# The mixer's input projection as 28 Strassen pairs in a stage of its own, with the delta rule beside the keys, the key fold and half the output projection

## The chip, the cores and the metric

The kernel runs on one NeuronCore of one Trainium2 chip. The metric is the time of one execution in microseconds (us). Time before: a median of 2743.02 us over three runs (2742.67 to 2745.15). TensorE (PE) multiplies matrices into PSUM, VectorE (DVE) and ScalarE (ACT) work on elements, GpSimd (POOL) does some element work and issues DMAs from software, SyncE (SP) issues DMAs. Each engine works through its own instructions in order and waits for the others by semaphores.

## What is computed

One layer of a streaming encoder on 512 tokens of width 2048, in float32: a token mixer, cross-attention to 256 memory tokens, and a feed-forward block with a short convolution. Cut to what matters here:

```python
h = rmsnorm(x, mix_norm)
proj = h @ w_mix_in                   # q, k, v, z (1024 each), 16 gate columns, 3 x 1024 of the short convolution
qkv = silu(causal_dwconv(proj[..., :3 * W], conv_w))
o = gated_delta_rule(l2norm(q), l2norm(k), v, g, beta)          # 8 heads x 128
y_gdn = rmsnorm(o, out_gain) * silu(z)
y_sc = b_gate * causal_dwconv(c_gate * h2, sc_conv)             # 1024 channels
x = x + concatenate([y_gdn, y_sc]) @ w_mix_out
x = x + memory_xattn(rmsnorm(x), rmsnorm(mem), w_q, w_k, w_v, w_o)
x = x + conv_ffn(rmsnorm(x), w_up, ffn_conv, w_down)
return rmsnorm(x, final_norm)
```

The delta rule carries a state of 128 x 128 for each head over the tokens. It is computed in chunks, with a unit lower triangular system to be solved in each. The kernel takes chunks of 128 tokens, four for each head.

## The kernel before

**Precision.** A float32 operand is split into a rounded part hi (type fp32r) and a rest lo. `wpiece` loads a piece of weights of 128x1024 (512 KB) on SP's queue, casts it on ScalarE (L143) and subtracts on VectorE (L144). `mm3` multiplies with three matmuls (hi hi, hi lo, lo hi; L154 to L156). Where the moving operand has only 256 columns, its hi and lo stand side by side in 512: one matmul over 512 columns and one over 256 then do the same (`mm2s`, L169 and L172).

**Stages**, in the order in which TensorE meets them:

1. `mem_proj(w_xk)`: keys of the memory tokens. The first pieces are loaded in parts by a hand-written order.
2. The key fold: `w_xq` times the keys, so that scores later need one product. The result goes to `wk_d`. The loads of x (POOL's queue) and its sums of squares stand beside it.
3. `mem_proj(w_xv)`: values, with the norm of x beside it.
4. The output fold: values times `w_xo`, to `mo_d`. Beside it the normed x is split into `hs`, and `gate_rows` computes the gate columns.
5. The mixer's input projection: 56 tiles of 128 columns. `wproj` gives each 16 x 3 matmuls over 512 columns. Four tiles for each head (`qkvz`), then 24 tiles for the short convolution.
6. The mixer's output projection, 16 tiles with K = 2048 (`proj`).
7. Scores and softmax; the attention's output (`out_proj`), with `up_prepare` beside it, which makes the seven operands of stage 8.
8. The up-projection in 44 Strassen pairs: two tiles of weights times both halves of the tokens, K in two halves. Seven products of 8 x (512 + 256) columns stand for eight of 8 x 3 x 256. The sums of weights are made in part by accumulating DMAs on POOL's queue (`pair_loads`), in part on VectorE.
9. The down-projection, also in Strassen form, and the final norm.

**The delta rule** of a head is a generator, `delta(h, ...)`. `weave` puts it on a list, and `tick` runs after every three matmuls of `wproj`: it adds 0.65 us to a written clock and takes the next step of each chain whose delay has passed. A step yields its own cost on TensorE and the delay until the next. So the order of the delta's matmuls among the products is fixed when the program is written, by these estimates. A head treats its four chunks at once in one tile of 128x512; a chunk's diagonal blocks of 32x32 are inverted by 31 steps of substitution on VectorE (L612, L613), over 128 partitions and 4 columns each (`G = 8` groups), with a round trip through memory before (`nd_d`) and after (`xd_d`), both on SP's queue. The recurrence then goes through the four chunks with tiles of 128x128. Outside of regions marked `manual_schedule`, a list scheduler orders the instructions of each engine by their place in the program and by their operands' readiness.

**Buffers.** 64 tiles of 128x512 (`tp`), five raw pieces of weights (`WST`), three of each split part, eight PSUM banks (3 `PM`, 5 `PG`).

## Time and profile before

| what | us |
|---|---|
| median of three runs | 2743.02 |
| the profiled execution | 2746.9 |
| its span, first to last instruction | 2745.1 |
| granted TensorE clock, mean | 0.998 |
| TensorE busy | 2719.1 |
| VectorE busy | 2101.1 |
| ScalarE busy | 1422.3 |
| the mixer's input projection (372 to 1078 us of the span) | 706.0 |
| the up-projection (1441 to 2308 us) | 867.0 |

Busy times are those of the trace; a matmul's mean duration (0.39 us for 512 columns) overlaps with the next one's, so that spacings are read from start to start.

### The profile page before, as it was taken

The page shows a single profiled execution, that of the slowest core. Times are in us where ns is not written, and L with a number is a line of the kernel's source. Part 1 is how long each engine was busy: PE and PEld are TensorE (multiplying, and loading weights), DVE is VectorE, ACT ScalarE, POOL GpSimd, SP SyncE. Part 2 cuts the span into 40 slices and gives each one's busy share as a digit, 9 for nine tenths or more (in the row PEclk, how much of TensorE's full clock was granted, in tenths as well). Part 3 has the DMA queues.
Part 4 walks back from the last instruction along what each step waited for, and adds up shares of the span by engine and source line. Part 5 has one row for each costly group of instructions (what it writes and reads, how often), then busy time and mean ns, then how long its engine had stood idle before and what let it go on. Part 6 is the DMA issues. An engine that isn't in the chain of part 4 may idle for free.

```text
span 2745.1 us, 38051 instructions
## 1 busy us (share of the span) xinstructions
PE 2719.1 (99%) x14045; PEld 2298.6 (84%) x14045; DVE 2101.1 (77%) x3342; ACT 1422.3 (52%) x2086; POOL 267.4 (10%) x258
## 2 busy tenths in 40 slices
PE   9999999999999999999999999999999999999998
PEld 8888788888788888888788888888888888888786
DVE  7777547878775324445679999999999999878878
ACT  6674644345443323224566656565656555554445
POOL 2120001012110000110020000000000000000201
PEclk9999999999999999999999999999999999999999
DMA  7786863333322234445566676767676776864976
GB/s 266 235 292 198 253 197 100 111 96 93 108 92 91 90 102 138 146 150 169 169 177 170 175 198 177 197 170 195 181 193 175 190 186 203 257 190 148 273 252 180
DMA packets 215851, 479.35 MB, mean 175 GB/s; under 512 B 28768, under 2 KB 96112, under 8 KB 215664
## 3 DMA queue, kind: packets, MB, share of 16 engines
q1 hardware_dynamic: 156320, 372.28, 41.9%
q0 software_dynamic: 20272, 62.94, 13.1%
q10 hardware_dynamic: 39072, 41.69, 4.3%
q8 instruction: 110, 1.80, 0.3%
q14 instruction: 77, 0.63, 0.1%
HBM read 424.13 MB, written 52.71 MB: 174 GB/s over the span
## 4 chain that ended last, share of the span: by engine, by line
PE 66%; DVE 2%; DMA 1%; issue 1%; ACT 1%; ACTq 0%; SPq 0%; DVEq 0%
PE px L169 12%; PE px L172 6%; PE pz L169 6%; PE psd L1232 4%; PE psd L1231 4%; PE psd L1230 4%; PE pssc L154 3%; PE psx L155 3%; PE psx L154 3%; PE psx L156 3%; PE pssc L156 3%; PE pssc L155 3%; PE pz L172 3%; PE py L169 3%; PE py L172 1%; PE pss L782 1%
## 5 line engine op out<-in xcount | busy, mean ns | idle before, releaser
L144 DVE TENSOR_TENSOR wlo<-wst,whi 128x1024 fp32r<-128x1024 f32 x316 | 393.0, 1245 | 283.5 <-ACT whi L143 280.4
L143 ACT CAST whi<-wst 128x1024 fp32r<-128x1024 f32 x316 | 331.5, 1049 | 516.0 <-PE pssc L155 143.9
L169 PE MATMUL px<-xo,whi 128*128 128x512 f32 x1400 | 352.7, 394 | 2.9 <-DVE ub L1149 2.9
L169 PEld LDWEIGHTS px<-xo,whi 128*128 128x128 f32 x1400 | 252.8, 190 | 48.9 <-DVE ub L1149 3.1
L863 ACT CAST whi<-wst 128x1024 fp32r<-128x1024 f32 x177 | 185.7, 1051 | 206.7 <-PE pz L169 119.8
L1232 PE MATMUL psd<-wlo,hdh 128*128 128x512 f32 x616 | 241.7, 392 | 3.4 <-DVE wlo L990 3.2
L1230 PE MATMUL psd<-whi,hdh 128*128 128x512 f32 x616 | 240.7, 391 | 0.1
L1231 PE MATMUL psd<-whi,hdl 128*128 128x512 f32 x616 | 240.6, 391 | 0.0
L864 DVE TENSOR_TENSOR wlo<-wst,whi 128x1024 fp32r<-128x1024 f32 x177 | 215.9, 1220 | 1.7 <-ACT whi L863 1.7
L172 PEld LDWEIGHTS px<-xo,wlo 128*128 128x128 f32 x1400 | 191.3, 191 | 13.8
L172 PE MATMUL px<-xo,wlo 128*128 128x256 f32 x1400 | 195.5, 283 | 0.0
L169 PE MATMUL pz<-xo,whi 128*128 128x512 f32 x704 | 176.6, 393 | 0.5 <-ACT whi L863 0.5
L863 ACT CAST whi<-s 128x1024 fp32r<-128x1024 f32 x131 | 136.3, 1040 | 78.3 <-PE px L169 42.6
L987 ACT CAST whi<-wst 128x1024 fp32r<-128x1024 f32 x99 | 104.3, 1053 | 122.8 <-issue 55.2
L864 DVE TENSOR_TENSOR wlo<-s,whi 128x1024 fp32r<-128x1024 f32 x131 | 159.9, 1221 | 0.4 <-ACT whi L863 0.4
L154 PE MATMUL psq<-hh,whi 128*128 128x512 f32 x384 | 155.7, 406 | 0.0
L154 PE MATMUL pssc<-hh,whi 128*128 128x512 f32 x384 | 153.3, 399 | 0.0
L156 PE MATMUL psq<-hh,wlo 128*128 128x512 f32 x384 | 150.3, 391 | 0.0
L156 PE MATMUL pssc<-hh,wlo 128*128 128x512 f32 x384 | 150.0, 391 | 0.0
L155 PE MATMUL psq<-hl,whi 128*128 128x512 f32 x384 | 149.9, 390 | 0.0
L155 PE MATMUL pssc<-hl,whi 128*128 128x512 f32 x384 | 149.8, 390 | 0.0
L169 PEld LDWEIGHTS pz<-xo,whi 128*128 128x128 f32 x704 | 126.6, 189 | 23.2 <-ACT whi L863 0.7
(369 smaller groups left out, 5924.1 us busy)
## 6 DMA issues: line engine op xcount, KB each, us to landing
wst<-in_w_up SPq DMA_DIRECT2D x132, 512.0 KB, 4.1
wst<-in_w_dn SPq DMA_DIRECT2D x121, 512.0 KB, 4.5
wst<-in_w_mix SPq DMA_DIRECT2D x112, 512.0 KB, 3.5
s<-in_w_up POOLq DMA_DIRECT2D x87, 512.0 KB, 6.0
s<-in_w_up SPq DMA_DIRECT2D x43, 512.0 KB, 4.5
hid<-hf_d SPq DMA_DIRECT2D x77, 256.0 KB, 5.2
wst<-in_w_xq SPq DMA_DIRECT2D x32, 512.0 KB, 5.0
wst<-in_w_xv SPq DMA_DIRECT2D x32, 512.0 KB, 3.8
```

The costliest lines, as they stand in the source:

```text
L143: nc.scalar.copy(hi, st)
L144: nc.vector.tensor_tensor(lo, st, f(hi), op=ALU.subtract)
L154: nc.tensor.matmul(ps, wh, xh, start=first, stop=False)
L155: nc.tensor.matmul(ps, wh, xl, start=False, stop=False)
L156: nc.tensor.matmul(ps, wl, xh, start=False, stop=last)
L169: nc.tensor.matmul(ps, hi[:, k * P : (k + 1) * P], x, start=first and k == 0, stop=False, skip_group_check=True)
L172: nc.tensor.matmul(ps[:, n:], lo[:, k * P : (k + 1) * P], x[:, :n], start=False, stop=end, skip_group_check=True)
L863: nc.scalar.copy(hi, t)
L864: nc.vector.tensor_tensor(lo, t, f(hi), op=ALU.subtract)
L1230: nc.tensor.matmul(ps, xh, wh, start=first, stop=False)
L1231: nc.tensor.matmul(ps, xl, wh, start=False, stop=False)
L1232: nc.tensor.matmul(ps, xh, wl, start=False, stop=last)
```

## The change

1. **Order of the stages.** Values first (with the loads and the norm of x beside them), then the output fold, the input projection, and only then keys and key fold, with the delta rule beside these.
2. **The input projection as 28 pairs.** The functions of the up-projection (`up_prepare`, `pair_loads`, the first pair's `begin_parts` and `begin_products`, `quad_left`, `quad_right`) are taken out of stage 8 and used by both. `up_prepare` for the mixer stands beside the output fold. Twelve pairs are those of the short convolution, sixteen those of q, k and v, z of the eight heads. Their results go to memory (`qkvz_d`, `ysc_d`), on ScalarE's queue. No step of the delta rule is woven in here, except for the gates.
3. **The delta rule by chunks of four heads.** A tile holds one chunk of four heads; `prepare_chunk` and `solve` are chains of their own for each of 2 x 4 (half of the heads, chunk), `invert` does the substitution for all 16 blocks of a half at once (`G = 2`, 16 columns on a partition), `recur` the recurrence with tiles of 128x512, `scaled` the norm and the gate. q, k, v, z and the decay are read back from memory on POOL's queue, pieces of 512 bytes, q and k twice.
4. **What it stands beside.** Keys (as before, 16 tiles), the key fold with three matmuls over 256 columns in place of one over 512 and one over 256, and the half of the output projection that needs only the short convolution; its sum with x goes to `xp_d`. The other half comes after the chains.

```diff
-G = 8
+G = 2
...
-    order = [(t, i) for t in tiles for i in range(2)]
...
+    def place(cost):
+        owed[0] += cost
+        if owed[0] > 0.6:
+            due, owed[0] = owed[0], 0.0
+            tick(due)
...
-        kts = mem_proj(g["w_xk"], True)
+        vts = values(g["w_xv"], beside_values)
...
+    def quad_left(pos, blocks, first, *between):
+        if pos:
+            a11, a12, a22, s1, s3 = pair_loads(blocks, pos)
+            w1 = wsplit(a11)
+            px = PG("px")
+            product(px, w1, 1, True)
...
+        product(px, wsplit(s2), 6, False)
...
+        product(pz, wsplit(s1), 5, True)
...
+    def quad_right(pos, left, whole):
+        a12, a22, s2, s3, px, pz, ga, gb, ub = left
+        product(px, wsplit(s3), 7, False)
+        tt(ub, px, ub, op=ALU.add)
...
+        product(pz, wsplit(a12), 3, False)
+        tt(gb, pz, gb, op=ALU.add)
+        if whole:
+            tt(ga[:, HI], gb[:, LO], gb[:, HI], op=ALU.add)
...
+        product(px, wsplit(a22), 4, False)
...
+    for i in range(0, 8, 2):
+        quads += [(40 + i, 48 + i, "ch", i), (41 + i, 49 + i, "ch", i + 1), (32 + i, 33 + i, "b", i)]
+    for h in range(H):
+        quads += [(4 * h, 4 * h + 1, "qk", h), (4 * h + 2, 4 * h + 3, "vz", h)]
...
+    ready_at = (0, 1, 3, 5, 7, 8, 10, 12)
...
+            if step in ready_at:
+                k = ready_at.index(step)
+                if k % 2:
+                    gate_rows(k // 2)
+                up_prepare(xts[k], xts[k + HK])
...
+    for pos, (_, _, kind, i) in enumerate(quads):
...
+        left = quad_left(pos, mix_blocks(pos) if pos else None, first, nothing, run_tails, nothing, nothing)
+        ga, _, ua, _ = quad_right(pos, left, True)
+        left_tail(kind, i, ga, ua)
+        tails.append((kind, i, ga, ua))
+        if pos > 1:
+            next(gate_steps, None)
+    run_tails()
...
+    def prepare_chunk(hb, j):
...
+        gb, k, q = load_decay(hb, j), load4("k", 1, hb, j), load4("q", 0, hb, j)
+        yield 0, 6.0
...
+    def invert(hb):
+        while prepared[hb] < 4:
+            yield 0, 1.0, 0
...
+        for m in range(B - 1):
+            r, n = B - 1 - m, min(m + 1, CB)
...
+            nc.vector.tensor_tensor(t, am, x[:, :n, m : m + 1].broadcast_to([P, n, r]), op=ALU.mult)
+            nc.vector.tensor_tensor(x[:, :n, m + 1 :], x[:, :n, m + 1 :], t, op=ALU.subtract)
+            if m % 4 == 3:
+                yield 0, 5.5, 0
+        nc.sync.dma_start(xd_d[hb].rearrange("j n b (g c) r -> (j n b g) c r", g=G), x)
+        for j in range(4):
+            weave(solve(hb, j), 4.0 + 8.0 * j)
+        weave(recur(hb), 30.0)
...
+            if j:
+                pr = PG("pr")
+                four(pr, ke[i], st)
+                nc.vector.tensor_tensor(r, r, pr, op=ALU.subtract)
+                yield 0.9, 2.5
...
+    order += [g["w_xk"][n, i] for n in range(KT) for i in range(2)]
+    order += [g["w_xq"][i, q] for i in range(KT) for q in range(2)]
+    order += [g["w_mo"][n, 1] for n in range(KT)]
+    for hb in range(2):
+        for j in range(4):
+            weave(prepare_chunk(hb, j), 4.0 + 10.0 * j + hb * 80.0)
+        weave(invert(hb), 20.0 + hb * 85.0)
...
+            for hh in range(2):
+                dst = ps[:, hh * NMEM : (hh + 1) * NMEM]
+                for k in range(4):
...
+                    nc.tensor.matmul(dst, hi[:, c], kt[:, :NMEM], start=k == 0, stop=False, skip_group_check=True)
+                    place(0.12)
+                    nc.tensor.matmul(dst, hi[:, c], kt[:, NMEM:], start=False, stop=False, skip_group_check=True)
+                    place(0.12)
+                    nc.tensor.matmul(dst, lo[:, c], kt[:, :NMEM], start=False, stop=k == 3, skip_group_check=True)
+                    place(0.12)
...
+    yp = [split(loaded(ysc_d[i]), "yp") for i in range(8)]
+    for n in range(KT):
+        ps = out_row(n, yp)
...
+        nc.sync.dma_start(xp_d[n], x0)
     while chains:
         tick(1.0)
...
+    order += [g["w_mo"][n, 0] for n in range(KT)]
+    yp = [split(loaded(y_d[h]), "yp") for h in range(H)]
```

More of the change, by code (lines that the diff above doesn't have):

```diff
@@ L367, in mem_proj, with load_x @@
             held = []
-            if beside:
-                beside(n2)
-        return out
+            beside(n2)
+        return out
+    xacc = cpool.tile([P, S], F32, tag="xacc", name="xacc")
+    xts, r0 = [], []
+    def load_x(n):
+        for _ in range(n):
+            i = len(xts)
+            xts.append(T("x0"))
+            nc.gpsimd.dma_start(xts[i], g["x"][i])
+            add_squares(xacc, xts[i], i == 0)
+    HK = KT // 2
+    S2 = S // 2
+    LO, HI = slice(0, S2), slice(S2, S)
@@ new lines, in gate_rows, with open_pool, TB @@
+    def gate_rows(m):
+        for n, k in enumerate((2 * m, 2 * m + HK, 2 * m + 1, 2 * m + 1 + HK)):
+            nc.tensor.matmul(psba[n * B : (n + 1) * B], wba[:, k], xts[k], start=m == 0, stop=m == 3, skip_group_check=True)
+    tt = nc.vector.tensor_tensor
+    tbs, uss = [], []
+    def open_pool(kept, name, bufs, **more):
+        stack = ctx.enter_context(ExitStack())
+        kept[:] = [stack, stack.enter_context(tc.tile_pool(name=nm(name), bufs=bufs, **more))]
+    def TB(s, dt=F32):
+        return tbs[1].tile([P, S], dt, tag="tb", name=nm(s))
@@ new lines, in begin_parts, with begin_products, some @@
+    def begin_parts(first):
+        a11, a12, a22, s1, s3 = first
+        first += [wsplit(a11), wsplit(a12)]
+        tt(a11, s1, a11, op=ALU.subtract)
+        tt(a12, a12, a11, op=ALU.subtract)
+    def begin_products(first):
+        px, py = PG("px"), PM("py")
+        def some(ps, w, r, low, k0, k1):
+            dst, src = (ps[:, HI], LO) if low else (ps, slice(0, S))
+            for k in range(k0, k1):
+                nc.tensor.matmul(dst, w[low][:, k * P : (k + 1) * P], xop[r][k][:, src], start=low == 0 and k == 0, stop=low == 1 and k == HK - 1, skip_group_check=True)
+        bx, by = (px, first[5], 1), (py, first[6], 2)
+        for args, low, k0 in ((bx, 0, 0), (bx, 1, 0), (by, 0, 0), (bx, 0, HK - 1), (bx, 1, HK - 1), (by, 1, 0), (by, 0, HK - 1), (by, 1, HK - 1)):
+            some(*args, low, k0, HK if k0 else HK - 1)
+        first += [px, py]
@@ new lines, in recur @@
+            vn = T("vn")
+            nc.vector.tensor_tensor(v4(vn), v4(pv), bc(bk[i], P), op=ALU.mult)
+            if 0 < j < 3:
+                sn = T("st")
+                nc.vector.tensor_tensor(v4(sn), v4(st), bc(egl[:, j, H4], P), op=ALU.mult)
+            yield 0.9, 2.5
+            pso = PG("pso")
+            for n in range(4):
+                if j:
+                    nc.tensor.matmul(v4(pso)[:, n], v4(st)[:, n], v4(qd[i])[:, n], start=True, stop=False)
+                nc.tensor.matmul(v4(pso)[:, n], v4(vn)[:, n], v4(at[i])[:, n], start=j == 0, stop=True)
@@ new lines, in trunk @@
+    mws.clear()
+    m2s.clear()
+    for i in range(KT // 2):
+        m2s.append(T("mem"))
+        nc.gpsimd.dma_start(m2s[i].rearrange("p (k m) -> p k m", k=2), g["mem"][2 * i : 2 * i + 2].rearrange("k p m -> p k m"))
+        mem_parts(i)
+    kts = []
+    for n in range(KT):
+        ps = PM("psk")
+        for i in range(2):
+            hi, lo = piece()
+            for k in range(8):
+                nc.tensor.matmul(ps, hi[:, k * P : (k + 1) * P], mws[8 * i + k], start=i == 0 and k == 0, stop=False, skip_group_check=True)
+                place(0.23)
+            for k in range(8):
+                nc.tensor.matmul(ps[:, NMEM:], lo[:, k * P : (k + 1) * P], mws[8 * i + k][:, :NMEM], start=False, stop=i == 1 and k == 7, skip_group_check=True)
+                place(0.12)
+        kts.append(mem_out(ps, 0))
```

736 lines of the change are left out of this document (370 added, 366 removed).

## The prediction

> **What bounds the kernel now.** I read the page's first part, then the busy time by stretch, then what TensorE waited for.
>
> ```profile
> span 2745.1 us, 38051 instructions
> PE 2719.1 (99%) x14045; PEld 2298.6 (84%) x14045; DVE 2101.1 (77%) x3342; ACT 1422.3 (52%) x2086; POOL 267.4 (10%) x258
> ```
>
> TensorE (PE) is busy 99% of the span. Matmuls are pipelined here, so that alone says little; the list of waits says more (engine, line, whom it waited for: total us, times, longest).
>
> ```profile
> PE psd L1232 <- DVE wlo L990: 3.2, 5, 1.6
> PE px L169 <- DVE ub L1149: 2.9, 1, 2.9
> PE pso L670 <- ACT vn L666: 2.7, 1, 2.7
> ...
> PE pv L664 <- DVE cv L661: 1.1, 2, 0.9
> ```
>
> The longest total is 3.2 us in 2745. PE is the bound in every stage, and its time is the number of its instructions times their spacing. The spacing is read from starts, not from mean durations. Here are the stretches (start:end, length, then busy us and count of PE, PEld, DVE, ACT, POOL; granted clock, DMA share, GB/s):
>
> ```profile
> 99.70:190.20 90.50, 90.50 (x515) 78.31 (x515) 68.36 (x98) 67.25 (x113) 25.25 (x26) 1.00 0.91 300
> 190.20:280.00 89.80, 89.80 (x512) 78.64 (x512) 68.27 (x100) 47.18 (x68) 0.00 (x0) 1.00 0.62 199
> 280.00:372.00 92.00, 92.00 (x420) 72.53 (x420) 51.42 (x52) 59.25 (x81) 0.00 (x0) 1.00 0.88 265
> 372.00:794.00 422.00, 418.32 (x2276) 346.45 (x2275) 326.49 (x798) 185.35 (x316) 56.84 (x49) 1.00 0.36 103
> 794.00:1078.00 284.00, 283.07 (x1385) 234.25 (x1385) 118.25 (x195) 89.33 (x119) 9.31 (x8) 1.00 0.32 103
> 1078.00:1252.00 174.00, 174.00 (x769) 144.14 (x769) 81.04 (x74) 54.12 (x71) 24.01 (x14) 1.00 0.45 145
> 1343.00:1441.00 98.00, 96.50 (x455) 79.01 (x455) 71.01 (x133) 64.53 (x136) 25.12 (x16) 1.00 0.58 166
> 1441.00:2308.00 867.00, 863.39 (x4931) 758.73 (x4929) 828.54 (x1192) 519.38 (x672) 74.08 (x87) 1.00 0.69 184
> ```
>
> The rows are the key fold, the value projection, the output fold, the mixer's input projection (two rows), its output projection, the attention's output, and the FFN's up-projection, which is already in Strassen pairs. DMA is near its limit only in the first (0.91, 300 GB/s).
>
> **The products.** The output projection is 16 tiles of 48 matmuls over 512 columns, all alike: 174.0 / 768 = 0.2266 us each. The input projection is 56 tiles of 48 such: 2688 x 0.2266 = 609.1 us. Its two stretches are 706.0 us, so 96.9 us there are not products: the delta rule's own matmuls and what their weaving costs. The up-projection has 44 pairs in 867.0 us, 19.70 us a pair. Seven products of this shape make a pair:
>
> ```profile
> 1495.62 2.00 PE L169 MATMUL pz<-xo,whi 128*128 128x512 f32 x8
> 1497.46 1.11 PE L172 MATMUL pz<-xo,wlo 128*128 128x256 f32 x8
> 1498.41 2.00 PE L169 MATMUL px<-xo,whi 128*128 128x512 f32 x8
> ```
>
> From start to start one product takes 2.79 us, seven take 19.5; 19.70 holds the seams too. An input pair has the same K of 2048, the same two tiles and the same 512 tokens. So 28 x 19.70 = 551.6 us take the place of 609.1: **57.5 us less**. This needs VectorE (DVE) to keep up. It is busy 828.54 / 44 = 18.8 us a pair in the up stage, so what an input pair adds after its products decides:
>
> ```profile
> L1048 DVE SCALAR_TENSOR_TENSOR ucv<-uu,cols,ucv 128x510 f32<-128x510 f32 x43 | 32.1, 747 | 0.0
> L1059 DVE TENSOR_TENSOR uu<-ub,rsy 128x256 f32<-128x256 f32 x43 | 18.1, 420 | 0.0
> L1074 DVE TENSOR_TENSOR h<-ucv,ucv 128x512 f32<-128x512 f32 x22 | 15.2, 690 | 0.0
> L1094 DVE TENSOR_TENSOR s<-h 128x256 f32<-128x256 f32 x21 | 8.9, 423 | 0.0
> ```
>
> The up pair ends with four norm multiplications (1.68), four convolution steps (2.99), a product (0.69) and half of four sums (0.85): 6.2 us. The change's query-key pair ends with six convolution steps and two gatings, 6 x 0.747 + 2 x 0.69 = 5.9; the value-gate pair with 3.6, the short-convolution pairs with 2.2 and 1.4. The seven splits and the other sums are the same. All four kinds stay below what the up stage carries without a loss. The queues too are those of the up stage: two accumulating loads a pair on POOL's, stores on ScalarE's (ACT) behind the DVE result, as there. If this cover went, each microsecond a pair would be 28.
>
> **What moves.** The preparation of the seven operands stands beside the output fold: 8 times seven subtractions and four sums of 256 columns at 0.42 us, 37 us of DVE, and the 16 splits of h that stand there now are gone (0.69 each, 11 us). The fold's 51.42 becomes about 82 with the first pair's parts, in 92. The attention's output carries the same preparation now at 71.01 in 98, and its 1.5 us of idle PE lie elsewhere (the softmax), so I take nothing for it. The loads of x go beside the first projection, now that of values; key projection and key fold go behind the mixer; the key fold uses three matmuls of 256 columns (0.95 / 8 = 0.119 us each, from the starts above: 1497.46 to 1498.41) for one of 512 and one of 256. 768 x 0.119 = 91.4 for 90.4: **1 us more**. The output projection is cut in two halves with the same 768 matmuls; its sum goes through memory, 16 loads and stores more beside a DMA share of 0.45: nothing.
>
> Seams: the memory tokens can be loaded for the keys only when operands of the last pair come free. The first eight are last read by the first product, 16.8 us (six products) before the end.
>
> ```profile
> mem<-in_mem SPq DMA_DIRECT2D x8, 256.0 KB, 6.9
> ```
>
> 6.9 us to land, then 16 casts and 16 multiplications: just in time. Bounds 0 to 8 us, and I take **2**, near the low end because the waits above hardly show a seam.
>
> **The delta rule.** Its matmuls are as many as before; four heads of one chunk stand where four chunks of one head stood. Of the 96.9 us some is the way back from its matmuls:
>
> ```profile
> 425.07 0.47 PE L154 MATMUL psq<-hh,whi 128*128 128x512 f32 x1
> 425.39 0.40 PE L155 MATMUL psq<-hl,whi 128*128 128x512 f32 x1
> ```
>
> The first matmul after a switch takes 0.32 us to the next start, 0.09 more than usual. A head makes 19 such blocks (152 in all), and a chunk of four heads 11 (86). If none ran together, that saves 66 x 0.09 = 6 us. The idle PE in the two stretches is 706.0 - 701.4 = 4.6. I leave the 96.9 as it is: fewer switches against longer steps to wait for (DVE's steps between them are four heads wide, 0.69 us at 512 columns). Ends: 6 + 4.6 = 10.6 less, or as much more as the second rival says.
>
> DVE gains. The substitution is 496 small operations now:
>
> ```profile
> L612 DVE TENSOR_TENSOR tm<-ab,xb 128x124 f32<-128x124 f32 (+30 forms) x248 | 66.1, 267 | 8.3 <-DMA ab<-nd_d 1.9
> L613 DVE TENSOR_TENSOR xb<-xb,tm 128x124 f32<-128x124 f32 (+30 forms) x248 | 62.9, 253 | 6.9
> ```
>
> It becomes 2 x 62 of up to 256 elements, about 154 on average. 0.25 us at a mean of 64 elements and 0.42 at 256 (L1059) put this at 0.33: 124 x 0.33 = 41 us for 129.
>
> Does the chain end in time? By the delays written in the generators, and counting 0.69 us for three matmuls as the code does, the last store of y is put at 237 of the 270 us of products that the keys, the key fold and half the output rows make. The other half waits for it, with 33 us in hand.
>
> **The sum.** -57.5 + 1 + 2 = -54.5 us. The profiled execution took 2746.9 us, 1.8 over its span of 2745.1; its time by the sum is 2692.4. The median of the runs shown is 2743.02, so I take the sum from that: **2688.5 us**. About 0.2% is what a measurement of this kernel can tell from no change.
>
> **Rivals.** *First: the pairs run at DVE's pace.* DVE is in the up stage at 828.54 of 867, and a query-key pair has its two convolutions in one lump instead of two. If the lump delays a split by 1 us in each of the 16 query-key and value-gate pairs, that is 16 us: 2704.5. For it: the single 2.9 us wait of px for ub. Against it: one such wait in 44 pairs.
>
> *Second: DVE falls behind beside the keys.* DVE now has the delta rule over 706 us; it gets it over some 350. The value stretch above shows its load for a projection, 68.27 less 16 norm multiplications of 0.69: 57 in 89.8. The first 56 us of keys (four prepared chunks, by the delays) hold 36 of that, 16 scalings of the memory tokens (16 x 0.48, 8), and four preparations:
>
> ```profile
> L279 DVE SCALAR_TENSOR_TENSOR mw<-mem,cols,mw 128x256 fp32r<-128x256 f32 x14 | 6.0, 481 | 1.7 <-ACT mw L278 1.7
> ```
> ```profile
> L546 DVE SCALAR_TENSOR_TENSOR dt<-gb,gc,mk 128x128 f32<-128x128 f32 x32 | 10.9, 378 | 0.0
> L578 DVE SCALAR_TENSOR_TENSOR nt<-pskk,bk,dts 128x128 f32<-128x128 f32 x32 | 9.7, 345 | 0.7
> L596 DVE TENSOR_REDUCE ndc<-nd 128x128 f32<-128x512 f32 x8 | 8.7, 1085 | 0.2
> ```
>
> These three make 29.3 / 8 = 3.7 us a chunk, three operations over 512 columns 2.1 and four small ones about 1: 7 in all. That is 72 for 56 and the 5 us that the delta's matmuls take there. GpSimd adds to it:
>
> ```profile
> 460.60 1.82 POOL L549 TENSOR_TENSOR dts<-dt,mk 128x512 f32<-128x512 f32 x1 [40.08 <-ACT dt L547]
> 462.38 1.31 POOL L552 TENSOR_TENSOR qd<-gb,cv 128x512 f32<-128x512 f32 x1
> ```
> ```profile
> 461.30 1.20 DVE L612 TENSOR_TENSOR tm<-ab,xb 128x64 f32<-128x64 f32 x1
> 462.53 1.24 DVE L613 TENSOR_TENSOR xb<-xb,tm 128x64 f32<-128x64 f32 x1
> ```
>
> Two operations of 0.23 us took 1.2 while GpSimd multiplied. One such hold for each of four chunks adds 4 us: 76 for 61, less the 5.6 us of the two pieces that are split ahead: 9 us late, and as much again in the second batch beside the key fold: 18 in all, 2706.5. The page "SBUF — State Buffer" of the Trainium skill (Who interferes with whom) says that VectorE and GpSimd share one pair of ports, held by one instruction at a time while the other blocks. The trace agrees (1.20 for 0.23 us), and by that rule each of the 40 GpSimd operations, all within some 350 us now, speaks for this rival.
>
> *Third, slower: the one SP queue.* Weights and the delta's round trips through memory stand in one line, and an issue that waits for its data holds up the weights behind it:
>
> ```profile
> SPq L698 <- POOL y L697: 38.5, 7, 6.1
> SPq L597 <- DVE ndc L596: 22.6, 6, 8.5
> SPq L602 <- DMA nd_d<-ndc: 16.9, 7, 3.9
> SPq L616 <- DVE xb L613: 13.3, 4, 4.1
> SPq L618 <- DMA xd_d<-xb: 5.5, 4, 2.4
> ```
>
> The change has 8 stores of y (5.5 us each), 8 of nd (3.8), 4 loads of ab (2.4), 2 stores of xd (3.3), 8 loads of it (1.4): 44 + 30 + 10 + 7 + 11 = 102 us of a held queue within some 300, where they were spread over 706. Five buffers, 14 us of pieces, cover a hold of 9. If that cover is gone, all 102 come on top: 2790. It is slower from 54 us, when more than half is bare. Against it: none of these holds shows as a wait of PE now.
>
> *Fourth: nothing gained.* If a matmul of 256 columns cost as much as one of 512 among these operands, a pair would take 112 x 0.2266 = 25.4 us; the starts quoted show 0.119. Something of this size would have to eat just the gain: 2743.
>
> **Chances.** Forecast 0.66, first 0.09, second 0.15, third 0.06, fourth 0.04. Faster: the first three, 0.90; within 0.2%: 0.04; slower: 0.06. The low end is the sum with the 10.6 us of the delta rule and the 2 of the seams gained, 2688.5 - 12.6 = 2676. The high end takes in either rival with the seams' 6 us more, and a little for both at once: 2715.
>
> **What would show it.** Right: a stretch of 28 pairs near 552 us with DVE near 18 us or less a pair; keys, key fold and half the rows in about 365 us with under 10 us of PE idle. The forecast is wrong if the waits of PE name a split (wlo, whi) in the pairs (first rival) or beside the keys (second), or a weight's load behind an SP issue (third), or if the products' starts are not 0.23 and 0.12 us apart (fourth).

## The result and the profile after

The changed kernel takes 2768.01 us (median of four runs, 2767.95 to 2768.06), the kernel before 2743.43 (2742.67 to 2745.15): a ratio of 1.0089 with a 95% interval of 1.0071 to 1.0106. It is **slower by 0.9%**, where 2688.5 us and 0.90 for faster had been forecast; the range ended at 2715. All times are medians of executions at the usual clock; of the experiments below, e1 has no stage times, because its profiled execution was a slow one (granted clock 0.65).

The page's first part for the changed kernel, and two of its 40-slice rows (tenths of busy time and of the granted clock):

```profile
span 2766.2 us, 40270 instructions
...
PE 2675.9 (97%) x14749; PEld 2307.3 (83%) x14749; DVE 2280.4 (82%) x3323; ACT 1585.1 (57%) x2301; POOL 367.4 (13%) x371
...
PE   9599999999989898999999999999999999999998
...
PEclk9799999999999998999999999999999999999999
```

TensorE's busy time fell by 43 us (2719.1 to 2675.9), and the span grew by 21. So the work did get less, and TensorE stands still now: a hole in the second slice, smaller ones in the stage of the keys, and there the granted clock is down as well. The busy time by stretch shows which stage has them: values, output fold, pairs with the seam behind them, keys to output rows, the rest (columns as in the prediction).

```profile
0.00:138.90 138.90, 103.42 (x530) 86.89 (x531) 82.13 (x128) 75.18 (x120) 41.67 (x42) 0.86 0.58 190
138.90:235.80 96.90, 93.92 (x418) 73.56 (x417) 72.73 (x128) 67.44 (x121) 1.77 (x2) 0.98 0.83 257
235.80:791.50 555.70, 549.04 (x3147) 482.69 (x3145) 476.95 (x600) 323.57 (x414) 53.65 (x65) 1.00 0.69 185
791.50:1273.60 482.10, 455.37 (x3009) 403.71 (x3010) 332.41 (x552) 260.18 (x428) 133.43 (x117) 0.96 0.65 210
1273.60:2766.20 1492.60, 1474.15 (x7651) 1260.40 (x7649) 1316.20 (x1918) 858.74 (x1222) 136.90 (x145) 1.00 0.69 193
```

Beside it stands what the forecast amounts to, stage by stage, from the stretches of the kernel before (99.7 is its first projection; 551.6 + 2; 89.8 + 91.5 + 174.0 + 96.9; 2745.1 - 1252.0):

| stage | forecast us | measured us | over |
|---|---|---|---|
| values | 99.7 | 138.9 | +39.2 |
| output fold | 92.0 | 96.9 | +4.9 |
| 28 pairs and the seam | 553.6 | 555.7 | +2.1 |
| keys, key fold, output rows, delta rule | 452.2 | 482.1 | +29.9 |
| rest | 1493.1 | 1492.6 | -0.5 |
| span | 2690.6 | 2766.2 | +75.6 |

The gain of the products is there; two stages gave it back, and 21 us more. What TensorE waited for, as shown of before (engine, line, whom it waited for: total us, times, longest):

```profile
PE psn L255 <- POOL xacc L264: 24.7, 1, 24.7
PE pskt L760 <- DMA k<-qkvz_d: 12.4, 4, 6.8
PE psk L172 <- DVE kt L334: 7.8, 1, 7.8
PE psk L990 <- DVE mw L280: 7.2, 2, 6.7
PE psx L157 <- ACT yph L152: 3.6, 2, 3.4
```

(psn is the row sum of x's squares; xacc collects these squares; k, pt, v and bt are operands of the delta rule; kt are copies of the values' results; mw is the split of the memory tokens, yph that of the output rows' operands, whi and wlo the two parts of a weight.) Before, the longest total was 3.2 us. Now one product, the row sum of x's squares (psn), waits 24.7 us for GpSimd, the transposition of the delta rule's k waits 12.4 for a load, and the first keys 6.7 for the memory tokens. None of these three was in the forecast's sum, apart from 2 us for the last.

GpSimd's timeline beside the values shows how the first comes about (start, us, engine, line, operation; in brackets the idle time before and its releaser):

```profile
35.38 1.82 POOL L381 DMA_DIRECT2D x<-in_x  x3
67.18 1.28 POOL L264 TENSOR_TENSOR xacc<-xacc,sq 128x512 f32<-128x512 f32 x1 [29.98 <-ACT sq L263]
68.41 0.56 POOL L381 DMA_DIRECT2D x<-in_x  x1
69.52 1.72 POOL L264 TENSOR_TENSOR xacc<-xacc,sq 128x512 f32<-128x512 f32 x1 [0.55 <-ACT sq L263]
...
110.47 1.26 POOL L264 TENSOR_TENSOR xacc<-xacc,sq 128x512 f32<-128x512 f32 x1 [0.27 <-ACT sq L263]
```

The loads of x (L381) and the additions of their squares (L264) are in one queue, in order. Three loads go out at 35; the next stands behind an addition that waits 30 us for ScalarE, which in its own order takes the first square at 65.9, behind casts and results of the values. From 67 on each load waits for an addition, which waits for the square of an earlier x: 15 additions from 67.2 to 111.7, one every 3.1 us. The 7.8 us for kt belong to the same loop: on ScalarE a square waits for its x, and the copy of a finished tile of values stands behind it.

```profile
77.72 0.63 ACT L263 ACTIVATE sq<-x 128x512 f32<-128x512 f32 x1 [2.02 <-DMA x<-in_x]
78.26 0.35 ACT L332 COPY kt<-psk 128x256 f32<-128x256 f32 x1
```

The stretches show that nothing else is short:

```profile
90.00:100.00 10.00, 0.00 (x0) 0.00 (x0) 0.95 (x2) 2.78 (x5) 6.03 (x7) 0.53 0.35 127
100.00:110.00 10.00, 0.00 (x0) 0.00 (x0) 2.02 (x5) 3.26 (x7) 5.73 (x8) 0.50 0.35 106
```

TensorE is idle, VectorE nearly so, the DMA share is 0.35, and the clock falls to half.

Beside the keys it is the same queue. The loads for the next chunk (gb, k, q) stand behind the multiplication dts of the chunk before, which waits for ScalarE and then itself takes up to 3.8 us, where the kernel before had at most 2.27:

```profile
814.51 2.14 POOL L785 TENSOR_TENSOR dts<-dt,mk 128x512 f32<-128x512 f32 x1 [36.43 <-ACT dt L783]
816.60 0.57 POOL L772 DMA_DIRECT2D gb<-gc_d  x1
817.17 0.76 POOL L767 DMA_DIRECT2D k<-qkvz_d  x1
817.91 0.76 POOL L767 DMA_DIRECT2D q<-qkvz_d  x1
826.90 3.79 POOL L785 TENSOR_TENSOR dts<-dt,mk 128x512 f32<-128x512 f32 x1 [8.23 <-ACT dt L783]
```

### The profile page after: what moved, and what is told of

The parts are those of the page before. It is cut to its first block, busy times and chain, and to the rows that moved or that the text cites. A ratio compares the mean times of both kernels' runs of the same rounds, so it can differ in the third digit from the quotient of the medians.

```text
span 2766.2 us, 40270 instructions
## 1 busy us (share of the span) xinstructions
PE 2675.9 (97%) x14749; PEld 2307.3 (83%) x14749; DVE 2280.4 (82%) x3323; ACT 1585.1 (57%) x2301; POOL 367.4 (13%) x371
## 4 chain that ended last, share of the span: by engine, by line
PE 80%; issue 7%; DMA 4%; DVE 4%; POOL 2%; ACT 2%; SPq 0%; ACTq 0%; POOLq 0%; DVEq 0%
PE px L172 19%; PE px L175 10%; PE pz L172 9%; PE pz L175 5%; PE py L172 5%; PE psd L1403 4%; PE psd L1401 4%; PE psd L1402 4%; PE psx L158 3%; PE psx L157 3%; PE psx L159 3%; PE py L175 2%; PE pss L1077 1%; PE pss L1079 1%; PE pss L1078 1%
## 5 line engine op out<-in xcount | busy, mean ns | idle before, releaser
L172 PE MATMUL px<-xo,whi 128*128 128x512 f32 x2288 | 573.9, 393 | 1.3 <-DVE ub L561 1.3
L172 PEld LDWEIGHTS px<-xo,whi 128*128 128x128 f32 x2288 | 411.5, 189 | 76.2 <-DVE ub L561 1.7
L467 DVE TENSOR_TENSOR wlo<-wst,whi 128x1024 fp32r<-128x1024 f32 x290 | 352.7, 1217 | 21.0 <-ACT whi L466 20.9
L146 ACT CAST whi<-wst 128x1024 fp32r<-128x1024 f32 x204 | 213.7, 1050 | 234.3 <-issue 65.9
L147 DVE TENSOR_TENSOR wlo<-wst,whi 128x1024 fp32r<-128x1024 f32 x204 | 258.5, 1273 | 97.1 <-ACT whi L146 94.8
L175 PEld LDWEIGHTS px<-xo,wlo 128*128 128x128 f32 x2288 | 312.1, 190 | 22.3
L175 PE MATMUL px<-xo,wlo 128*128 128x256 f32 x2288 | 319.0, 282 | 0.0
L1199 ACT CAST whi<-wst 128x1024 fp32r<-128x1024 f32 x99 | 104.3, 1054 | 122.3 <-issue 55.2
L175 PEld LDWEIGHTS pz<-xo,wlo 128*128 128x128 f32 x1152 | 157.2, 190 | 11.2
L175 PE MATMUL pz<-xo,wlo 128*128 128x256 f32 x1152 | 160.6, 282 | 0.0
L1403 PEld LDWEIGHTS psd<-wlo,hdh 128*128 128x128 f32 x616 | 115.6, 188 | 30.1 <-DVE wlo L1202 6.2
L172 PE MATMUL py<-xo,whi 128*128 128x512 f32 x560 | 140.2, 392 | 0.0
L1202 DVE TENSOR_TENSOR wlo<-wst,whi 128x1024 fp32r<-128x1024 f32 x99 | 121.0, 1222 | 19.1 <-ACT whi L1199 16.8
L1402 PEld LDWEIGHTS psd<-whi,hdl 128*128 128x128 f32 x616 | 115.6, 188 | 24.0
```

The costliest lines, as they stand in the source:

```text
L146: nc.scalar.copy(hi, st)
L147: nc.vector.tensor_tensor(lo, st, f(hi), op=ALU.subtract)
L172: nc.tensor.matmul(ps, hi[:, k * P : (k + 1) * P], x, start=first and k == 0, stop=False, skip_group_check=True)
L175: nc.tensor.matmul(ps[:, n:], lo[:, k * P : (k + 1) * P], x[:, :n], start=False, stop=end, skip_group_check=True)
L467: tt(lo, t, f(hi), op=ALU.subtract)
L1199: nc.scalar.copy(hi[:, i * n : (i + 1) * n], t)
```

## The experiments

Theory: what was lost is two stages' waiting for GpSimd's one queue. Rivals: VectorE has too much to do there; GpSimd's arithmetic itself; the half clock behind each hole; the new places of weights and tokens. All runs in one table, by the first matmul of each stage in the profiled execution (us); the ratio is to the kernel before, run on the same chip:

| kernel | values | fold | pairs, seam | keys to rows | rest | median | ratio (95%) |
|---|---|---|---|---|---|---|---|
| changed | 138.9 | 96.9 | 555.7 | 482.1 | 1492.6 | 2768.01 | 1.0089 (1.0071 to 1.0106) |
| e1 | | | | | | 2752.05 | 1.0028 (1.0016 to 1.0041) |
| e2 | 140.2 | 96.7 | 555.7 | 471.1 | 1492.6 | 2751.51 | 1.0033 (1.0020 to 1.0046) |
| e3 | 140.5 | 96.8 | 553.4 | 482.6 | 1489.1 | 2767.41 | 1.0083 (1.0068 to 1.0098) |
| e4 | 117.7 | 99.0 | 554.0 | 474.0 | 1489.8 | 2737.55 | 0.9977 (0.9968 to 0.9987) |
| e5 | 117.3 | 96.5 | 554.8 | 475.3 | 1490.0 | 2736.32 | 0.9969 (0.9958 to 0.9980) |
| e6 | 138.8 | 96.8 | 555.4 | 481.8 | 1491.1 | 2765.10 | 1.0076 (1.0061 to 1.0091) |
| e8 | 126.4 | 93.7 | 553.6 | 479.4 | 1492.7 | 2746.61 | 1.0006 (0.9998 to 1.0015) |
| e9 | 117.8 | 94.3 | 553.4 | 473.7 | 1492.5 | 2731.62 | 0.9951 (0.9938 to 0.9963) |
| e10 | 117.2 | 94.9 | 553.4 | 488.1 | 1492.4 | 2747.91 | 1.0018 (1.0009 to 1.0027) |
| e11 | 105.5 | 104.6 | 553.4 | 472.9 | 1490.1 | 2730.43 | 0.9950 (0.9937 to 0.9964) |
| e12 | 99.8 | 93.4 | 555.4 | 370.5 | 1489.1 | 2610.33 | 0.9513 (0.9495 to 0.9530) |
| e13 | 103.8 | 104.3 | 553.6 | 473.2 | 1489.4 | 2728.15 | 0.9941 (0.9927 to 0.9955) |
| e14 | 103.9 | 100.3 | 553.4 | 473.3 | 1489.7 | 2723.84 | 0.9925 (0.9912 to 0.9939) |

(e7 is a variant of the kernel before.) The rest, which no edit touches, lies between 1489.1 and 1492.7 us, so a difference of 2 or 3 us in one stage says nothing.

**e1: x's loads ahead of the additions on GpSimd's queue.**

```diff
     def load_x(n):
-        for _ in range(n):
-            i = len(xts)
+        while len(xts) < KT:
             xts.append(T("x0"))
-            nc.gpsimd.dma_start(xts[i], g["x"][i])
+            nc.gpsimd.dma_start(xts[-1], g["x"][len(xts) - 1])
+        for i in range(squared[0], squared[0] + n):
             add_squares(xacc, xts[i], i == 0)
+        squared[0] += n
```

> All sixteen loads of x are issued on GpSimd's queue ahead of its additions of squares; nothing else differs from the changed kernel (2768.0 us). Theory A (a load of x stands behind an addition that waits for an earlier load, so that they come one by one, 2.8 us each): the loads all stand at about 36 to 46 us, the squares start at 66 as before and sixteen additions of 1.3 us end near 88, so that TensorE's wait of 24.7 us for xacc falls under 14 and the 7.8 us wait of the values ahead of it goes: 2740 to 2752. Rival B (the memory is too busy for x and the values' weights at once): the loads only move, the wait stays above 20 us: 2762 to 2770.

Measured 2752.05 us, 16.0 less, at the very end of the theory's range. The order in the queue is a cause; it is not all of the 39.

**e2: dts on VectorE.**

```diff
-        nc.gpsimd.tensor_tensor(v4(dts), v4(dt), mrep(M_STRU), op=ALU.mult)
+        nc.vector.tensor_tensor(v4(dts), v4(dt), mrep(M_STRU), op=ALU.mult)
```

> The multiplication dts is done on VectorE in place of GpSimd; nothing else differs from the changed kernel (2768.0 us). Theory A (the loads of the next chunk's keys stand on GpSimd's queue behind dts, which waits for the exponential): TensorE's waits for k and v from memory (12.4 and 2.2 us) go and with them two stretches of half clock: 2743 to 2756. Rival C (VectorE is too full beside the keys, the second rival of the prediction): 8 x 0.83 us more on VectorE makes it worse: 2770 to 2780.

2751.51 us, 16.5 less; keys to rows 11.0 less, and the wait for k is gone from the list. The stages are those of the longest of its five executions (2758.05 us). The stages that the edit doesn't touch differ by up to 1.3 us in the profile.

**e6: only the loads moved**, to ScalarE's queue; dts stays on GpSimd.

```diff
-        gb, k, q = load_decay(hb, j), load4("k", 1, hb, j), load4("q", 0, hb, j)
+        gb, k, q = load_decay(hb, j, nc.scalar), load4("k", 1, hb, j, nc.scalar), load4("q", 0, hb, j, nc.scalar)
```

> The loads of decay, keys and queries for prepare_chunk are issued on ScalarE's queue; dts stays on GpSimd; nothing else differs from the changed kernel (2768.0 us). Theory A (these loads stood behind dts on GpSimd's queue): the waits for k from memory go as they did with dts on VectorE: 2748 to 2758. Rival E (dts on VectorE helped because GpSimd's multiplication blocked VectorE): no gain, 2765 to 2770.

2765.1 us, in the rival's range; keys to rows 481.8, as before the edit. The waits:

```profile
PE pskt L760 <- DMA k<-qkvz_d: 5.8, 3, 2.9
PE pv L756 <- DVE pt L888: 4.8, 2, 4.1
PE pswk L1005 <- ACT wk L1012: 4.1, 2, 2.5
```

The wait for k halves, and the rest goes to the next results. But the edit did not bring the loads forward. On ScalarE's queue they stand behind ScalarE's own work: the second chunk's k goes out at 816.82 us, where the changed kernel issued it at 817.17 (shown above), and e2 at 780.46, before the keys begin (e6 first, then e2):

```profile
816.82 0.45 ACTq L767 DMA_DIRECT2D k<-qkvz_d  x1
```
```profile
780.46 0.75 POOL L767 DMA_DIRECT2D k<-qkvz_d  x1
```

So e6 tests neither the order of the loads nor its rival. How e2's gain divides between the loads' earlier issue and dts itself, which took 2.13 us in the median on GpSimd and takes 0.68 on VectorE, stays open:

```profile
L785 POOL TENSOR_TENSOR dts<-dt,mk x8: 1278/2130/3786, 814.5 to 934.8; 128x512 f32<-128x512 f32 x8
```
```profile
L785 DVE TENSOR_TENSOR dts<-dt,mk x8: 679/683/694, 816.3 to 927.4; 128x512 f32<-128x512 f32 x8
```

(The view of one tile, changed kernel and e2; min, median and longest in ns.)

**e3: the memory tokens' loads and splits ahead of the last pair's tails.**

```diff
+    ...
+    for i in range(KT // 2):
+        m2s.append(T("mem"))
+        nc.gpsimd.dma_start(m2s[i]..., g["mem"][2 * i : 2 * i + 2]...)
+        mem_parts(i)
     run_tails()
     uss[0].close()
```

> The loads and splits of the memory tokens for the keys stand ahead of the last pair's tail in the program; nothing else differs from the changed kernel (2768.0 us). Theory A (the splits wait on VectorE and ScalarE behind the tail of the last pair): the gap of 6.8 us at the seam falls under 3, and the 10 us of half clock behind it go: 2756 to 2763. Rival D (the tokens themselves land too late, because their buffers come free only in the last pair): no change, 2766 to 2769.

2767.41 us, in the rival's range, but not by its mechanism. The tokens were not late: in the changed kernel their loads went out between 767.9 and 775.3 us and landed in at most 5.1, so by 781. VectorE took their first split at 790.94, behind the convolution of the last pair. In e3 it is hardly earlier:

```profile
790.10 0.88 DVE L280 SCALAR_TENSOR_TENSOR mw<-mem,cols,mw 128x256 fp32r<-128x256 f32 x2
```

Their place in the program did not put the splits ahead of that tail in VectorE's order. The longest wait for mw falls from 6.7 to 4.6; a seam of some 5 us stays.

**e7: a hole alone**, in the kernel before: one matmul in the projection of the keys waits for a chain of 17 operations on VectorE.

```diff
+            if begin and n2 == 4:
+                a, b = T("gap"), T("gap")
+                nc.vector.tensor_copy(a, ps[1])
+                for _ in range(8):
+                    nc.vector.tensor_tensor(b, a, a, op=ALU.add)
+                    nc.vector.tensor_tensor(a, b, b, op=ALU.add)
+                nc.tensor.matmul(PM("gap")[:, :P], ones, a[:, :P], start=True, stop=True)
```

> The kernel before with one wait put into TensorE's order: in the key projection, one small matmul that needs a chain of 17 operations of VectorE over 512 columns, some 11 to 13 us after its first input is there; its result is not used. Theory A (an idle TensorE is followed by a stretch of half clock, so that it costs more than itself): the clock falls to 0.5 behind the gap and the time rises by the gap and 2 to 6 us more. Rival F (the half clock in the changed kernel belongs to something else, and a gap costs itself): the time rises by the gap alone and no half clock shows there.

2763.93 us, 19.5 over the kernel before (2744.46 on that chip).

```profile
PE gap L374 <- DVE gap L373: 18.4, 1, 18.4
```
```profile
66.00:84.60 18.60, 0.23 (x2) 0.02 (x1) 16.60 (x29) 2.75 (x8) 0.00 (x0) 0.58 0.17 55
84.60:89.60 5.00, 4.92 (x15) 4.15 (x16) 0.02 (x1) 0.63 (x1) 0.00 (x0) 0.50 0.02 3
89.60:95.00 5.40, 5.40 (x32) 4.72 (x32) 2.96 (x4) 1.79 (x4) 0.00 (x0) 1.00 0.30 97
```

Behind the hole the clock is 0.50 for 5 us: 15 matmuls, where the next 5.4 us have 32. The product behind the hole takes 4.93 us from start to start, where one takes 2.79 otherwise, so the half clock adds 2.1 us to the hole of 18.4:

```profile
85.13 3.76 PE L169 MATMUL psk<-mw,whi 128*128 128x512 f32 x8
...
90.06 2.00 PE L169 MATMUL psk<-mw,whi 128*128 128x512 f32 x8
```

The medians (19.5 us, 16 to 24 by the interval) agree, and are too coarse to say it. The hole itself is what counts.

**e12: both suspects taken away.** x's squares, row sum and norm are left out, and of the delta rule all but the reading of z, which is stored as y; the products and x's loads stay.

```diff
-            add_squares(xacc, xts[i], i == 0)
...
-            weave(prepare_chunk(hb, j), 4.0 + 10.0 * j + hb * 80.0)
-        weave(invert(hb), 20.0 + hb * 85.0)
+            weave(gate_only(hb, j), 100.0 + 10.0 * j + hb * 60.0)
```

> The changed kernel without the squares, row sum and norm of x beside the values (the loads stay where they are), and without the delta rule: y is z as it is read back. Theory (the whole excess beside the values and beside the keys comes from these two): values about 100 us, fold 92 to 97, pairs and seam 552 to 556, keys to output rows 452 less the delta rule's 97, 355, and the seam's 5 to 7: 358 to 364; the time 2600 to 2615. Rival (a part is the weights', the memory tokens' or the key fold's own, from its new place and form): one of these stages is longer by 8 us or more, the time over 2618.

2610.33 us, within the theory's range; but one stage misses its own:

```profile
0.00:99.80 99.80, 97.31 (x528) 83.59 (x529) 72.13 (x115) 61.04 (x100) 21.55 (x27) 1.00 0.78 270
99.80:193.20 93.40, 92.07 (x419) 72.46 (x418) 68.40 (x120) 67.13 (x121) 1.74 (x2) 1.00 0.83 262
193.20:748.60 555.40, 548.75 (x3146) 482.61 (x3144) 476.91 (x600) 323.77 (x414) 51.89 (x63) 1.00 0.69 184
748.60:1119.10 370.50, 361.72 (x2048) 317.85 (x2049) 195.76 (x220) 158.96 (x219) 29.59 (x21) 0.98 0.69 226
```
```profile
PE psk L994 <- DVE mw L280: 7.2, 2, 6.7
PE psx L157 <- ACT yph L152: 6.1, 1, 6.1
```

Values 99.8: the whole excess of that stage is x's squares and norm, not the sixteen loads by themselves, which are still made here, with no addition between them. Keys to rows 370.5, where 355.3 was forecast without the delta rule: 15.2 us are not its own. The largest part (9.6 us, in the output rows: 183.6 for 174.0) is a second seam, where these rows begin: they read the short convolution's results back behind their own weights on SP's queue, and TensorE waits 6.1 us for the first split. The delta rule cost 482.1 - 370.5 = 111.6 us, 14.7 more than the 96.9 of the prediction.

**e4: e1, e2 and e3 together**, the squares begun two steps earlier, and the stores of y on GpSimd's queue.

```diff
             if n2 < 2:
+                beside(n2)
                 continue
...
-            load_x({2: 6, 3: 6, 4: 4}[n2])
+        if n2 < 3:
+            load_x({0: 5, 1: 5, 2: 6}[n2])
...
-        nc.sync.dma_start(y_d[4 * hb : 4 * hb + 4, ...
+        nc.gpsimd.dma_start(y_d[4 * hb : 4 * hb + 4, ...
```

> The three edits together, the squares of x begun three tiles of values earlier, and the stores of y issued from GpSimd's own queue instead of SP's. Theory A (the loss lies in queues, not in the parts that the prediction priced): the 40 us of the values, 20 of the delta's waits and 10 of the seam go, so that it falls below the kernel before (2743): 2690 to 2712. Rival C (VectorE too full beside the keys): the values' part alone is won, 2725 to 2740.

2737.55 us: 30.5 less than the change, 0.23% less than before, and far from the 2690 to 2712 of the theory. The waits for xacc and for k are gone and mw's is at 4.6, but others appear or stay: VectorE's splits and additions at 3 to 6 us each (wlo, kt, pt), and yph at 5.5.

**e5: the squares added on VectorE and spread**, the norm too, and the delta rule's and the rows' loads earlier.

```diff
+    def square_x(i0, i1):
+        ...
+            nc.scalar.activation(sq, xts[i], AF.Square)
+            nc.vector.tensor_tensor(xacc, xacc, sq, op=ALU.add)
...
+        if i == 9:
+            ysl += [loaded(ysc_d[n]) for n in range(8)]
```

> As the run with the three edits together (2737.6 us), with these differences: the squares of x are added on VectorE instead of GpSimd and spread over five tiles of values, the loads of x go a batch ahead, the norm of x is spread over three tiles; the loads of the short convolution's rows stand halfway in the key fold, and solve's loads one step earlier. Theory A (the rest of the loss is single waits behind a queue, each with its stretch of half clock): the waits of 6.1, 4.9 and 4.4 us around the values and the 5.5 us wait for yph go: 2708 to 2722. Rival C (VectorE is too full in the values and beside the keys): TensorE's waits move to other splits, 2730 to 2742.

2736.32 us, the rival's range (VectorE's line is full). e8, e9 and e10 each change e5 in one point to see whose line it is.

**e8: the squares summed on TensorE**, 16 matmuls for 15 additions on VectorE.

```diff
-            nc.vector.tensor_tensor(xacc, xacc, sq, op=ALU.add)
+            nc.tensor.matmul(xsum[0], onesr, sq, start=xsum[1] == 0, stop=xsum[1] == KT - 1)
```

> The squares of x are summed on TensorE (16 matmuls more over 512 columns, 3.6 us) in place of 15 additions of 0.69 us on VectorE (10 us) in the stage of the values; the rest as in e5. Theory (VectorE's line is too long beside the values, and the row sum waits for the last of these additions: psn for xacc 7.1 us): the stage of the values falls from 117.3 to 104 to 110 us, the time from 2736 to 2723 to 2730. Rival (the line is no longer than it was; x still comes too late, or ScalarE's squares do): the stage stays at 115 to 121, the time at 2733 to 2740.

2746.61 us, slower than both expectations: values 126.4. VectorE has less to do, but TensorE now waits for ScalarE's squares in the middle of its products (psn for sq 5.3 us, and wlo 5.9). Taking work from VectorE is no help by itself; what is read, and when, matters more.

**e9: the delta rule's other four operations off GpSimd.**

```diff
-        nc.gpsimd.tensor_tensor(qd[i], gb, q, op=ALU.mult)
-        nc.gpsimd.tensor_tensor(k, gb, k, op=ALU.mult)
+        nc.vector.tensor_tensor(qd[i], gb, q, op=ALU.mult)
+        nc.vector.tensor_tensor(k, gb, k, op=ALU.mult)
...
-        nc.gpsimd.tensor_tensor(s1, s1, q, op=ALU.add)
-        nc.gpsimd.tensor_tensor(o, o, z, op=ALU.mult)
+        nc.vector.tensor_tensor(s1, s1, q, op=ALU.add)
+        nc.vector.tensor_tensor(o, o, z, op=ALU.mult)
```

> e5, with the delta rule's last four operations on GpSimd (qd, ke, the sum of s1 and q, o times z: 32 of 512 columns) on VectorE. Theory (GpSimd holds VectorE up while it works, so that VectorE's results beside keys and key fold come late): keys to output rows fall from 475 to 460 to 468 us, the time to 2721 to 2730. Rival (VectorE's own line is what is long there): 32 x 0.69 = 22 us more in that line, keys to output rows 478 to 490 us, the time 2738 to 2750.

2731.62 us, between the two: 22 us of work more on VectorE, and keys to rows 1.6 us shorter, not longer. On the whole VectorE is not full there, and GpSimd's share of what is left is small. The ratios' intervals (0.9938 to 0.9963, 0.9958 to 0.9980 for e5) just overlap.

**e10: every written delay of the delta rule times 1.25.**

```diff
-                    c[1] = clock[0] + held[1]
+                    c[1] = clock[0] + 1.25 * held[1]
```

> e5, with every written delay between steps of the delta rule times 1.25; by the written clock the last chain then ends at 264 of the 270 us of products, in place of 237. Theory (the written delays are shorter than the chip's, so that TensorE comes to the delta's matmuls before their operands are there: 13 us of its waits name pt, bt, v, st, ww, vn): keys to output rows fall from 475 to 460 to 467 us, the time to 2721 to 2729. Rival (the waits stem from bursts in VectorE's line, which come later but stay): 470 to 480 us, the time 2732 to 2742.

2747.91 us, slower than both. The waits for pt and v leave the head of the list, but another of the delta rule's operands joins it (ww, 5.3 us), and the end of the chains runs into the split of the output rows' operands:

```profile
PE psx L157 <- ACT yph L152: 13.6, 4, 8.1
PE pswk L1022 <- DVE wlo L147: 9.4, 2, 7.6
```

**e11: e9, with the row sum of x one tile later** and part of the norm beside the fold.

```diff
-        elif n2 == 5:
+        elif n2 == 6:
             r0.append(rstd_rows([xacc]))
...
+                if k > 4:
+                    norm_x(k, k + 1)
```

> e9, with the row sum of x a tile of values later in TensorE's order and the norm of the last three pairs of x tiles beside the output fold. Theory (what is left of the loss beside the values is the place of that product: TensorE comes to it 7.1 us before the last addition): the stage of the values falls from 117.8 to 107 to 112 us, the fold stays at 93 to 97, the time from 2731.6 to 2721 to 2727. Rival (VectorE's line is as long as before, so another result takes the wait over, a norm multiplication or a split): values and fold together stay at 208 to 214 us, the time 2728 to 2735.

Values fall to 105.5, the fold grows to 104.6: together 210.1 (212.1 in e9), the rival's case. The 7.1 us of psn turned into

```profile
PE psba L427 <- DVE xo L452: 10.8, 1, 10.8
```

the gates' columns, the next product that reads the end of the same line.

**e13: e11, with the gates' columns behind the preparation.**

```diff
-                if k % 2:
-                    gate_rows(k // 2)
                 up_prepare(xts[k], xts[k + HK])
+            if step in (5, 9, 12, 15):
+                gate_rows((5, 9, 12, 15).index(step))
```

> e11, with the matmuls of the gates' columns three steps of the output fold behind the preparation that they read (steps 5, 9, 12 and 15 in place of 1, 5, 8 and 12). Theory (VectorE has room beside values and fold; each wait there is a product of TensorE's that reads its line too early): the 10.8 us of psba go, values and fold together fall from 210 to 197 to 202 us, the time from 2730 to 2718 to 2723. Rival (VectorE has no room: with the preparation of x it needs more than the two stages last, so the wait goes to the next reader, the first pair's operands or a split): values and fold together 206 to 212 us, the time 2727 to 2733.

Together 208.1, again the rival's range, and the wait has moved on to a weight's split:

```profile
PE psmo L638 <- DVE wlo L147: 9.9, 1, 9.9
```
```profile
105.00:120.00 15.00, 5.14 (x22) 4.00 (x21) 14.66 (x29) 7.75 (x17) 0.00 (x0) 0.80 0.17 39
120.00:135.00 15.00, 15.00 (x59) 12.16 (x58) 14.96 (x31) 10.48 (x22) 0.00 (x0) 0.86 0.81 237
...
165.00:180.00 15.00, 15.00 (x70) 11.51 (x69) 10.00 (x15) 10.67 (x17) 0.00 (x0) 1.00 0.81 253
```

But the stretches speak against "no room": VectorE is at 29.6 of 30 us just behind the row sum, and at 10.0 of 15 later. It is a burst.

**e14: the same operations spread over the fold**, and its weights split one piece ahead.

```diff
-    ready_at = (0, 1, 3, 5, 7, 8, 10, 12)
+    ready_at = (1, 3, 5, 7, 9, 10, 12, 13)
...
-            fold_pieces(2 * step + 2)
+            fold_pieces(2 * step + 3)
...
-                if k > 4:
+                if k > 2:
                     norm_x(k, k + 1)
```

> e13, with the eight preparations of x spread over steps 1 to 13 of the output fold (0 to 12 before), the norm of five pairs of x tiles (three before) beside them, the gates' columns behind them, and the fold's weights split one piece ahead. VectorE has the same operations; from 165 us on it was busy 27.5 of 43 us in e13, from 105 to 135 us 29.6 of 30. Theory (VectorE has room over the two stages, and what is left is a burst behind the row sum): the 9.9 us of psmo for wlo fall below 3, values and fold together go from 208 to 198 to 202 us, the time from 2728 to 2717 to 2723. Rival (the line is too long as a whole, so the first pair's operands come late instead): 205 to 210 us, the time 2725 to 2732.

2723.84 us; values and fold 204.2, between the two ranges, and the wait for wlo 5.2 in place of 9.9. e11 and e13 only handed one wait on (7.1, 10.8, 9.9 us); this edit shortened it. That fits the burst, and a part is left. But the edit also splits the fold's weights one piece ahead, which helps wlo directly, and no run separates the two. This is the best version: 0.75% faster than the kernel before (0.61 to 0.88), 1.6% faster than the change as it was made.

## Why the prediction was wrong

**Right: the products.** 28 pairs took 549.0 us from the first product to the last (235.8 to 784.8 of the span), against 551.6, with VectorE at 463 us in 538 of them:

```profile
242.00:500.00 258.00, 258.00 (x1482) 226.97 (x1482) 208.00 (x261) 141.20 (x178) 22.88 (x27) 1.00 0.67 174
500.00:780.00 280.00, 280.00 (x1605) 246.35 (x1604) 254.92 (x324) 172.74 (x222) 30.21 (x37) 1.00 0.70 188
```

TensorE has no idle time in them. The first and the fourth rival are out, and the third nearly so: of SP's loads only the 3.4 us for yph are among the long waits.

**The step that failed first** is "The loads of x go beside the first projection, now that of values", which had no price at all. It cost 39.1 us in its stage and 3.5 in the fold (138.9 and 96.9 against 99.8 and 93.4 in e12). Before, loads and squares lay beside the key fold, and only the norm beside the values; nothing waited for the row sum. The loop of load, square and addition was there already: its 15 additions ran from 105.4 to 187.2 us, 82 us, and cost nothing because TensorE came to the sum at 190.2, at the end of the key fold. In the changed kernel they run from 67.2 to 111.7, and TensorE comes at 87.1. The trace of before could have priced that. The change put loads, squares, row sum, norm and the eight preparations into one chain through four engines, in some 190 us, with TensorE reading it at three places. The prediction summed VectorE's work (the fold "about 82, in 92") and didn't follow the chain. The sum was not too small: in e14 VectorE is busy 83.72 us in the fold, and the two stages need 204.2 us, where the changed kernel needs 235.8 with less work on VectorE. What was wrong is that cover was counted as time beside, and not as a result that is there when TensorE comes to read it.

**The second failed step** is "I leave the 96.9 as it is". The delta rule cost 111.6, and TensorE is idle for 26.7 of the stage's 482.1 us, where the prediction had set 10 as its sign. The second rival had said 18 us more for keys and key fold, by VectorE's falling behind, with GpSimd's holds in it; it got the place and nearly the size, 14.7, and not quite the mechanism. VectorE was at 69% of that stage, and at 12.92 of 20 us where TensorE waited longest (820 to 840); it was full from 880 to 904 (23.76 of 24), where TensorE did not wait; and 22 us more on it (e9) cost nothing. What was late was a chain: exp on ScalarE, dts on GpSimd, and behind it in the same queue the loads of the next chunk. At the longest wait for k (6.8 us) dts ends at 830.69, the load goes out at 831.21, and TensorE has k at 836.71. With dts on VectorE (e2, one instruction a chunk moved) these waits go and the stage is 11.0 us shorter; what the loads' place and what dts's own time had in it is not separated. The rule that the prediction named (the Trainium skill, "SBUF — State Buffer", Who interferes with whom) is seen here from GpSimd's side: the dts of 3.79 us lies over three splits of weights, which VectorE did at its usual 1.2 us each, and ends 1.1 us after the last of them.

```profile
826.07 3.49 DVE L147 TENSOR_TENSOR wlo<-wst,whi 128x1024 fp32r<-128x1024 f32 x3
```

By that page of the Trainium skill the one that issues first blocks the other; the prediction had priced only GpSimd blocking VectorE. Moving the remaining 32 GpSimd operations to VectorE gained 1.6 us in the stage (e9), no more than the stages differ by without an edit.

**Seams, mis-sized.** The term was 2 us with bounds of 0 and 8. The seam behind the pairs measured 6.7 (the row below). The prediction had priced the landing of the tokens and 16 casts and multiplications behind it; the tokens were there by 781 us, but their splits stood behind the last pair's convolution on VectorE (e3). The switch from key fold to output rows, which the prediction didn't list, measured 6.1 in e12 and 3.4 in the changed kernel. Together with the clock behind them and smaller waits, keys to rows is 15.2 us longer without any delta rule.

```profile
791.48 6.31 PE L990 MATMUL psk<-mw,whi 128*128 128x512 f32 x15 [6.66 <-DVE mw L280]
```

**The sum afterwards**: x's chain 39.1 + 3.5, the fold itself 1.4, pairs and seam 2.1, delta rule 14.7, keys to rows without it 15.2, rest -0.5: 75.5 of the 75.6 us. No rival on the slower side was the one that came. The chance of 0.06 for slower rested on SP's queue alone; GpSimd's queue, which the change fills as well (267.4 us busy before, 367.4 after), was looked at for the ports, and for two loads a pair, and not for what stands behind what.

**Open**: what is left in keys to rows. e14 has 473.3 there, e12's 370.5 and the priced 96.9 make 467.4; no run tells apart the waits of 2 to 5 us that are left (mw, pt, wlo, wk, bt). Whether e1's 16.0 would be more with the squares earlier is in e4, but not by itself. e2's gain and e14's are each of two possible causes, as said there.

## What to carry to other kernels

A stage that is moved takes its companions with it: for each, write down who issues it, what it stands behind in that engine's order, and at which product its result is read, and price the wait there; a sum of busy time below the stage's length proves nothing about when the last of it is done. On an engine that issues loads and computes, a load waits for the arithmetic ahead of it and for what that waits for; put loads first. Another engine's queue helps only if that engine's own work doesn't hold them as long (e6), so look in the trace at when they go out. When a mended wait only moves to the next reader of the same chain, look at the stretches for a burst beside a lull, and try spreading the work: e14 did that, and split its weights earlier, and was the one edit here that shortened such a wait.

## What the runs showed of the hardware

- Holes of some us halve the granted clock here: to 0.53 and 0.50 in the two stretches of the hole from 90 to 110 us, and for 5.5 us behind the 6.66 us of the seam, 13 matmuls in 5.5 us (0.42 us each, for 0.2266):

```profile
791.50:797.00 5.50, 5.50 (x13) 4.33 (x14) 2.80 (x7) 2.44 (x6) 0.00 (x0) 0.50 0.13 48
```

The mean clock went from 0.998 to 0.982. The Trainium skill ("TensorE: Matmul & The Clock Gate", Part 1) gives a window of about 3.4 us, idle or busy, after which the clock changes; the 5 to 5.5 us here are longer than one such window and shorter than two. In e7 the half clock added 2.1 us behind its hole; for the changed kernel no run separates it from the holes.

- A GpSimd multiplication of 128x512 took 1.28 to 3.79 us within one run, the same operation on VectorE (e2) 0.68 to 0.69 each time.
